# Stores, low parts, norms and reloads moved within the attention and gate stages of a hybrid encoder block

## The chip, the cores and the metric

The kernel runs on one core of a Trainium2 chip. The metric is the device time of one execution in microseconds (us). The engines of the core run side by side, each working through its own queue in order: TensorE (PE in the profile; its weight loads are PEld), VectorE (DVE), ScalarE (ACT), GpSimd (POOL), and SyncE (SP), which here issues nearly all DMAs. An instruction that waits holds up everything behind it on its own queue and nothing else, except through the data and the buffers that others wait for.

## What is computed

One layer of a bidirectional hybrid encoder over 1024 tokens of width 1024, in float32:

```python
h = rmsnorm(x, norm_mix)
q, k, v, r, lr_f, lr_b, u, g_a, g_b = split(h @ w_in)
# branch A: gated linear attention, 4 heads, forward and backward scan, summed
log_a = log_sigmoid(lr @ w_decay_up + b_decay) / 16           # one for each direction
o = gla(q, k, v, log_a_f) + flip(gla(flip(q), flip(k), flip(v), flip(log_a_b)))
o = o * rsqrt(mean(o * o) + eps) * gla_norm                   # for each head
y_a = (o * silu(r)) @ w_branch_gla
# branch B: window means of u minus the token, a small product per group
merged = sigmoid(g_a) * y_a + sigmoid(g_b) * y_b
x = x + merged @ w_out
x = x + (silu(gate) * up) @ w_ffn_out                         # gate, up = rmsnorm(x) @ w_ffn_in
out = rmsnorm(x, norm_final)
```

## The kernel before

**Products.** Every float32 matrix product is made of three matmuls on operands that are split into a high part (`hi`, a cast on ACT) and a low part (`lo`, source minus `hi`, on DVE or POOL): `hi*hi`, `lo*hi`, `hi*lo` (`split_to`, L200 to L202; `products`, L270 to L273). A group of three is called a unit here. After each group `mm3` calls `pump` (L162), which issues whatever side work has come due: steps put off by `soon(delay, step)` (a first-in first-out list, counted in units), weight splits in `pending`, a list `aside` of jobs that run beside the products, and `side`, generators that issue the attention. So the order of each queue is fixed when the program is written, and a unit on PE is the clock by which the other engines' work is dealt out.

**Larger products** such as the projections of r, of the gates and of the feed-forward part run in a form with seven block products instead of eight (`p` = 1 to 7). It needs sums of blocks of the weights and of the activations beforehand. `branch_jobs` and `r_jobs` make such sums of weights on POOL (the tiles `wsum` and `rraw`, recorded at L755), store them to DRAM (L736) and are dealt out by `prepare_beside(jobs, every, ...)` (L767): one step for each `every` units, only while no weight split is pending, and with `floor` as the limit for how far a late job list may catch up. A job's store is issued three steps after the job.

**Heads.** For head 0 to 3 the loop at L1186 makes q and k (`project_qk`, L882) while the attention of the head before runs in `side`. After head 0 come three value products and `store_block`, which writes one block of the features to DRAM so that its buffers can be used for other things; then the two job lists are started (L1198, L1199). After head 2 come the value products of heads 2 and 3.

**Attention of a head** (`attention`, L913). First the decays: four products `z`, for each a DVE step (`la`, L925) and an ACT step (absolute value, L926), then four exponentials (L931), then four logarithms (L940). Between these, the previous head's second half is finished (`unscaled`, L932 to L936): `norm` (L1092, two DVE instructions for each part) and `turn` (L1099, a DVE transpose), which lays out the head's output in a tile `ot` and puts four stores for each half on the list `deferred`. `flush` (L938) issues what is on that list on the SP queue: eight stores, four of the half that was turned in the loop and four of the half that was turned just before. Then come scans and exponentials (`decay`, `exponentials`, `apply_decay` with two POOL products, L985 and L986), the backward states, and the loop over eight chunks (L1118), which has on PE the output products and the next state, on DVE the state update (L1016) and the copy of the output (L1132), on ACT the scaled states (`sf`, L1023) and the sum of squares (L1133). At chunks 5, 6 and 7 of that loop the first half of the head's own output is normed and turned (L1145 to L1151). The last head isn't turned (L1100); its second half is normed after the loop by `soon` (L1156). That output is read much later, by `gated` in the first gate run.

**The r products** (L1399): 21 block products of 12 matmuls, n = 0 to 20, three units `u` for each of `p` = 2, 5, 3, 1, 6, 7, 4, beside the attention of the last head. Before each, `r_step` splits the weights that are needed four products later and loads those of seven later, and `r_event(n)` issues what is listed at L1380 to L1397. Each product's result is read out of its PSUM bank (`r_evict`, L1360) by ACT (L1369) or added by DVE (L1367); p = 5 needs the right-hand operand `right[5]`, a sum of features whose high part is cast by `cast_sum` (L699, ACT) and whose low part is made by `low_sum` (L704) as `trl`. That of p = 5 is put off from inside the k projection of the last head (L907). Three PSUM banks go round among the projections and the r products, so product n waits until the bank of three before has been read. Products 18 to 20 have p = 4 and add into the banks that p = 7 used, so each waits for the DVE addition of the product three before.

At events 14 to 23 the stored outputs of heads 0 to 2 are loaded again (`load_ol`), r rows go through a silu (`gate_row`) and are multiplied on DVE (L1313). At events 20 and 21 `load_block_again` fetches the block that `store_block` had put away, as high and low part (`hh`, `hl`), four loads of 512 KB. The first gate run follows the r products (its p order is 1, 5, 6, 3, 2, 7) and uses the reloaded block for p = 2.

**Buffers.** Most tiles of 4 KB for each partition share a pool of 39 slots; a DMA or a cast into a new tile waits until an earlier tile's last reader is done. Weight parts share pools of 4 raw and 6 split buffers.

Of the kernel before, what the change touches and what calls it, by code (L numbers as in the profile page):

```python
# [23 lines left out]
HEADS = 4  # L24
# [30 lines left out]
def kernel(  # L55
# [20 lines left out]
    nc = tc.nc  # L76
# [21 lines left out]
    def slot(dtype=F32, shape=(2, HALF), s="slot"):  # L98
        return slots.tile([P, *shape], dtype, tag="slot", name=name(s))
# [55 lines left out]
    def soon(delay, *steps):  # L155
        put_off.extend([delay, step] for step in steps)
# [101 lines left out]
    def take(ahead=True):  # L258

        if not ready:  # L260
            prepare()
        w = ready.pop(0)
        w.finish()
        if ahead:
            prepare()
        return w
# [291 lines left out]
    def later(dst, src):  # L558
        deferred.append((dst, src))

    def flush(eng=nc.sync):
        while deferred:
            eng.dma_start(*deferred.pop(0))
# [78 lines left out]
    def r_jobs():  # L642
        raws = {}
        todo = [(u, c) for u in range(TRIO + 1) for c in range(2)]

        def load_rows_of(u, c):
            raws[u, c] = slot(s="rraw")
            for j in range(2):
                k0, c0 = (4 * j + 2 * c) * P, R0 + 2 * u * P
                nc.sync.dma_start(  # L650
                    raws[u, c][:, j, :].rearrange("p (k x) -> p k x", k=2),
                    w_in[k0 : k0 + 2 * P, c0 : c0 + 2 * P].rearrange("(k p) x -> p k x", p=P),
                )

        yield partial(load_rows_of, *todo[0]), None, None
        for n, (u, c) in enumerate(todo):
            if n + 1 < len(todo):
                yield partial(load_rows_of, *todo[n + 1]), None, None
            halves = [raws[u, c][:, j, :].rearrange("p (k x) -> p k x", k=2) for j in range(2)]
            a11, a12, a21, a22 = (halves[j][:, :, i * P : (i + 1) * P] for i in range(2) for j in range(2))  # L660
            for op, dst, a, b, p in (
                (padd, a22, a21, a22, 5), (psub, a21, a11, a21, 7), (psub, a11, a22, a11, 6), (psub, a12, a12, a11, 3)
            ):
                yield partial(op, dst, a, b), None, r_out[u][p][:, 2 * c : 2 * c + 2, :]
# [29 lines left out]
    def load_sums(p):  # L694
        sums_in[p] = [slot(F32R, s="trl")[:, :, :] for _ in range(2)]
        for c, t in enumerate(sums_in[p]):
            nc.sync.dma_start(as_f32(t), f_out[p][:, c])
# [69 lines left out]
    def prepare_beside(jobs, every, put=PUT, lag=1, quick=0, floor=-1e9):  # L767
        aside.append([beside(chain(*jobs), every, put, lag, quick), 1 if quick else every, floor])
# [97 lines left out]
    def r_step():  # L866
        n = next(r_steps, None)
        if n is not None:
            r_split(n)
            r_load(n + 3)  # L870
        return n is not None
# [10 lines left out]
    def project_qk(h, last=False):  # L882
        q = slot(s="q")
        k = slot(s="k")
        for dst, scale in ((q, DK**-0.5), (k, 1.0)):
            final = last and dst is k
            w = take(not final)
            if final:
                value_weights[0].splits(2)
            elif last:  # L890
                value_weights.append(ValueWeights())
            begun = h == HEADS - 1 and dst is k
            if begun:
                load_sums(5)
                for _ in range(2):
                    r_step()
            for half in range(2):
                ps = feature_major(w, hT, half)
                nc.scalar.activation(dst[:, half, :], ps[:, :], AF.Copy, scale=scale)
                if begun:  # L900
                    r_step()
                    if half == 0:
                        load_sums(6)
                        for c in range(2):
                            cast_sum(5, c)
                        for c in range(2):
                            soon(4 + 2 * c, partial(low_sum, 5, c))  # L907
                elif h == HEADS - 1 and half == 0:
                    for n in range(3):
                        r_load(n)  # L910
        qk_heads[h] = q, k

    def attention(h):  # L913
# [21 lines left out]
        if unscaled:  # L935
            unscaled.pop(0)()  # L936
        yield 1.5
        flush()  # L938
        for run in runs:
            nc.scalar.activation(zs[run][:, :], zs[run][:, :], AF.Ln, bias=1.0)  # L940
        yield 6.5

        totals = {}

# [147 lines left out]
        def norm(half, part):  # L1092
            for i in range(2 * part, 2 * part + 2):
                t = o[half][:, i, :]
                nc.vector.scalar_tensor_tensor(
                    t, t, scales[half][:, i : i + 1], gain_row[:, :], op0=ALU.mult, op1=ALU.mult
                )

        def turn(half, part):  # L1099
            if h == HEADS - 1:  # L1100
                return
            if part == 0:
                turned[half] = slot(shape=(DV // SQ, 4 * SQ), s="ot")
            two = slice(2 * part, 2 * part + 2)
            nc.vector.transpose(
                turned[half][:, :, :].rearrange("p k (n b) -> p n k b", b=SQ)[:, two],
                o[half][:, two, :].rearrange("p n (k a) -> p n k a", a=SQ),
            )
            if part:
                to = o_out[h][half].rearrange("(k a) (i m) -> i a k m", a=SQ, i=4)  # L1110
                for i in range(4):
                    later(to[i], turned[half][i * SQ : (i + 1) * SQ, :, :])
# [5 lines left out]
        for n in range(NT):  # L1118
            half, i = n // 4, n % 4
            op = bank(ps_g, "op")  # L1120
            products(op[:, :DV], tokens(p, n), value(n), last=False)
            terms = []
            if n < NT - 1:
                terms.append((chunk_of(qe, n, 1), sb[half][:, i, :]))
            if n > 0:
                terms.append((chunk_of(qe, n, 0), sf[:, :]))
            for j, (a, b) in enumerate(terms):
                if j == len(terms) - 1 and n < NT - 1:
                    sf = s1((DV,), "sf")
                    old = advance(old, n, 0, kts[half, 0], sf[:, :], n == NT - 2)  # L1130
                nc.tensor.matmul(op[:, :DV], a, b, start=False, stop=j == len(terms) - 1)
            nc.vector.tensor_copy(o[half][:, i, :], op[:, :DV])  # L1132
            nc.scalar.activation(  # L1133
                op[:, DV:], op[:, :DV], AF.Square, scale=1.0 / 16.0, accum_out=ms[:, n : n + 1]
            )
            if n == 0:
                yield 0.38
                kts[1, 0] = transposed_keys(1, 0)
            if n == 1:
                yield 0.75  # L1140
                q_next = scores(1)
            if n == 3:
                p = q_next
                scales[0] = rms_scale(ms[:, :4], 4, "ors")
            if n == 5:  # L1145
                norm(0, 0)
            elif n == 6:
                turn(0, 0)
            elif n == 7:
                norm(0, 1)  # L1150
                turn(0, 1)  # L1151
            yield 1.02
        scales[1] = rms_scale(ms[:, 4:], 4, "ors")
        if h == HEADS - 1:
            o_heads[h] = o
            for part in range(2):  # L1156
                soon(3 + part, partial(norm_and_turn, part))
            return
        unscaled.extend(partial(norm_and_turn, part) for part in range(2))

# [25 lines left out]
    for h in range(HEADS):  # L1186
        if h:
            project_qk(h, h == 2)
        else:
            first_qk()  # L1190
            begin(attention(0))
        if h < HEADS - 1:
            begin(attention(h + 1))
        if h == 0:
            for ts in ((7,), (6,), (5, 4)):
                pair_products(ts)
            store_block()
            prepare_beside(map(branch_jobs, range(4)), 2.7)  # L1198
            prepare_beside([r_jobs()], 1.5, floor=-0.5)  # L1199
        if h == 2:  # L1200
            value_weights.pop().products()

# [170 lines left out]
    def event(n, *steps):  # L1373
        r_events.setdefault(n, []).extend(steps)
# [16 lines left out]
    for u in range(TRIO):  # L1391
        event(14 + u, partial(load_ol, u, 0))
        event(16 + u, partial(gate_row, u, 0))
        event(18 + u, partial(load_ol, u, 1))
        event(21 + u, partial(gate_row, u, 1))
    event(20, partial(load_block_again, 0))
    event(21, partial(load_block_again, 1))  # L1397

    for n, (u, p) in enumerate(r_products):  # L1399
        if n:  # L1400
# [826 lines left out]
    for at, p in enumerate(OUT_ORDER):  # L2227
# [9 lines left out]
        for i in range(CLOSE if closing else n_of):  # L2237
            n = at * n_of + i
# [57 lines left out]
```

## Time and profile before

| | |
|---|---|
| time, median of 3 runs | 1369.36 us (1368.5 to 1370.36) |
| profiled execution, its own time | 1369.4 us |
| its span, first to last instruction | 1367.7 us |
| DVE, ACT, POOL busy | 854.2, 652.0, 801.8 us |
| DMA | 268.24 MB, mean 196 GB/s |
| mean granted clock of TensorE | 0.997 |

The profile is one execution. A row of a timeline gives the start, the busy time, the engine, the line, the operation with its output and inputs, the count of merged instructions, and in brackets how long the engine had been idle before it and which instruction ended that wait. A row of a table of stretches gives for each engine the busy time and the number of instructions, then the granted clock, the share of the DMA engines' time and GB/s. A row of waits gives the total, the number and the longest in us. Start times of matmuls that follow each other without a gap lie some 0.23 us apart, though each is shown with 0.39 us, since they are pipelined.

### The profile page before, as it was taken

Reading aid. Unit: us, or ns where it says so; the run is one execution under the profiler, and the core shown is the slowest. Engines: PE = TensorE matmul, PEld = TensorE weight load, DVE = VectorE, ACT = ScalarE, POOL = GpSimd, SP = SyncE. Lnnn points to the kernel's source line nnn. Section 1 sums busy time; section 2 is a strip of 40 time slices with the busy share of each in tenths; the row PEclk is TensorE's granted clock in tenths of the full one; section 3 lists DMA queues with packets and bytes.
Section 4 is the critical chain, followed back from the end, with each engine's and each line's share of the span. In section 5 each row is a group of like instructions: output and inputs, shape, how many; then the busy total and the mean of one; then the engine's idle time right before and its main releaser. Section 6 shows DMA issues by size and latency. Waiting matters only on the chain. (4 is left out here: it accounts for less than half of the span.)

```text
span 1367.7 us, 17976 instructions
## 1 busy us (share of the span) xinstructions
PE 1350.2 (99%) x6226; PEld 1123.2 (82%) x6226; DVE 854.2 (62%) x1051; ACT 652.0 (48%) x1184; POOL 801.8 (59%) x608
## 2 busy tenths in 40 slices
PE   9999999999999999999999999999999999999998
PEld 7888887878788888888888888888888888888886
DVE  6975566567435767769874955565565556343375
ACT  7365665676434445554356533333333334444253
POOL 3332846385496547658764386666666667555454
PEclk9999999999999999999999999999999999999999
DMA  7343638454987669996426354555544447975561
GB/s 228 111 162 101 192 105 228 123 157 134 306 278 253 202 186 335 373 372 220 135 77 233 126 172 154 178 177 177 176 157 137 140 142 272 391 286 185 170 215 77
DMA packets 190139, 268.24 MB, mean 196 GB/s; under 512 B 12728, under 2 KB 112608, under 8 KB 190048
## 3 DMA queue, kind: packets, MB, share of 16 engines
q1 hardware_dynamic: 189904, 266.83, 58.3%
q8 instruction: 49, 0.80, 0.2%
q14 instruction: 42, 0.34, 0.1%
q10 hardware_dynamic: 144, 0.26, 0.1%
HBM read 178.70 MB, written 88.34 MB: 195 GB/s over the span
## 5 line engine op out<-in xcount | busy, mean ns | idle before, releaser
L202 POOL TENSOR_TENSOR wl<-fs,wh 128x512 fp32r<-128x512 f32 x120 | 166.2, 1388 | 155.2 <-ACT wh L201 97.9
L273 PE MATMUL ps<-gh,wh 128*128 128x512 f32 x616 | 240.8, 391 | 0.0
L273 PE MATMUL ps<-gl,wh 128*128 128x512 f32 x616 | 240.1, 390 | 0.3 <-DVE gl L1854 0.3
L273 PE MATMUL ps<-gh,wl 128*128 128x512 f32 x616 | 240.0, 390 | 0.0
L202 POOL TENSOR_TENSOR wl<-fraw,wh 128x512 fp32r<-128x512 f32 x90 | 129.6, 1440 | 62.1 <-ACT wh L201 59.7
L202 POOL TENSOR_TENSOR ol<-gor,oh 128x1024 fp32r<-128x1024 f32 (+1 forms) x42 | 101.8, 2428 | 85.5 <-ACT oh L201 70.3
L273 PEld LDWEIGHTS ps<-gl,wh 128*128 128x128 f32 x616 | 115.7, 188 | 24.3 <-DVE gl L1854 0.7
L273 PEld LDWEIGHTS ps<-gh,wl 128*128 128x128 f32 x616 | 115.7, 188 | 24.1
L273 PEld LDWEIGHTS ps<-gh,wh 128*128 128x128 f32 x616 | 115.8, 188 | 23.9 <-ACT hb L1873 0.2
L273 PE MATMUL ps<-hh,wh 128*128 128x512 f32 x296 | 120.3, 407 | 0.1
L273 PE MATMUL ps<-oh,ol 128*128 128x512 f32 x308 | 120.0, 389 | 0.0
L273 PE MATMUL ps<-ol,oh 128*128 128x512 f32 x308 | 119.9, 389 | 0.0
L273 PE MATMUL ps<-oh,oh 128*128 128x512 f32 x308 | 119.9, 389 | 0.0
L202 POOL TENSOR_TENSOR wl<-wraw,wh 128x512 fp32r<-128x512 f32 x56 | 93.3, 1696 | 44.2 <-ACT wh L201 39.3
L273 PE MATMUL ps<-hh,wl 128*128 128x512 f32 x296 | 116.0, 392 | 2.9 <-POOL wl L202 2.9
L273 PE MATMUL ps<-hl,wh 128*128 128x512 f32 x296 | 116.1, 392 | 0.8 <-DMA hl<-h_out 0.8
L202 DVE TENSOR_TENSOR ol<-wor,oh 128x1024 fp32r<-128x1024 f32 (+1 forms) x42 | 62.4, 1496 | 66.9 <-ACT oh L201 53.9
L273 PE MATMUL ps<-trh,wh 128*128 128x512 f32 x224 | 89.1, 398 | 1.9 <-ACT r L1369 1.9
L273 PE MATMUL ps<-trl,wh 128*128 128x512 f32 x224 | 87.3, 390 | 0.0
L273 PE MATMUL ps<-trh,wl 128*128 128x512 f32 x224 | 87.3, 390 | 0.0
L201 ACT CAST wh<-fs 128x512 fp32r<-128x512 f32 x120 | 73.7, 614 | 26.2 <-DVE fs L1223 25.1
L201 ACT CAST oh<-wor 128x1024 fp32r<-128x1024 f32 (+1 forms) x42 | 41.1, 978 | 63.9 <-PE ps L273 26.5
(286 smaller groups left out, 3148.2 us busy)
## 6 DMA issues: line engine op xcount, KB each, us to landing
fraw<-in_w_ffn_in_dram SPq DMA_DIRECT2D x44, 512.0 KB, 7.2
gor<-g_out SPq DMA_DIRECT2D x35, 512.0 KB, 4.9
g_out<-s SPq DMA_DIRECT2D x44, 256.0 KB, 2.4
fraw<-in_w_in_dram SPq DMA_DIRECT2D x20, 512.0 KB, 6.7
wor<-t_out SPq DMA_DIRECT2D x20, 512.0 KB, 4.8
g_out<-g SPq DMA_DIRECT2D x33, 256.0 KB, 2.5
x<-in_x_dram SPq DMA_DIRECT2D x16, 512.0 KB, 4.5
wor<-in_w_ffn_out_dram SPq DMA_DIRECT2D x15, 512.0 KB, 7.8
```

The source lines that it names most:

```text
L201: nc.scalar.copy(hi, src)
L202: eng.tensor_tensor(lo, src, as_f32(hi), op=ALU.subtract)
L273: nc.tensor.matmul(ps, a[i], b[j], start=first and n == 0, stop=last and n == 2, skip_group_check=onto)
```

## The change

Five edits, all in the order in which work is issued; no operation is added or taken out.

1. `flush` of the finished head's stores moves from before the logarithms to behind them and behind 6.5 more units.
2. The two low parts of `right[5]` go from DVE to GpSimd, put off by 3 and 6 units where it was 4 and 6.
3. In the last head the two norms of the first half leave the loop. All four parts are normed after it, at 4, 6, 8 and 10 units; the two of the second half were at 3 and 4.
4. The job lists are dealt out at another pace: `branch_jobs` every 1.6 units with a limit on catching up, where it was 2.7 without one; `r_jobs` every 1.2 where it was 1.5.
5. The block is loaded again at events 18 and 19 instead of 20 and 21; the second loads of `ol` and their rows move one event later.

```diff
@@ project_qk
                         for c in range(2):
-                            soon(4 + 2 * c, partial(low_sum, 5, c))
+                            soon(3 + 3 * c, partial(low_sum, 5, c, nc.gpsimd))
@@ attention
         yield 1.5
-        flush()
         for run in runs:
             nc.scalar.activation(zs[run][:, :], zs[run][:, :], AF.Ln, bias=1.0)
         yield 6.5
+        flush()
...
         def turn(half, part):
-            if h == HEADS - 1:
-                return
             if part == 0:
...
-            if n == 5:
-                norm(0, 0)
-            elif n == 6:
-                turn(0, 0)
-            elif n == 7:
-                norm(0, 1)
-                turn(0, 1)
+            if h < HEADS - 1:
+                if n == 5:
+                    norm(0, 0)
+                elif n == 6:
+                    turn(0, 0)
+                elif n == 7:
+                    norm(0, 1)
+                    turn(0, 1)
             yield 1.02
         scales[1] = rms_scale(ms[:, 4:], 4, "ors")
         if h == HEADS - 1:
             o_heads[h] = o
-            for part in range(2):
-                soon(3 + part, partial(norm_and_turn, part))
+            for part in range(4):
+                soon(4 + 2 * part, partial(norm, part // 2, part % 2))
             return
@@ the loop over heads
             store_block()
-            prepare_beside(map(branch_jobs, range(4)), 2.7)
-            prepare_beside([r_jobs()], 1.5, floor=-0.5)
+            prepare_beside(map(branch_jobs, range(4)), 1.6, floor=-0.5)
+            prepare_beside([r_jobs()], 1.2, floor=-0.5)
@@ the events of the r products
     for u in range(TRIO):
         event(14 + u, partial(load_ol, u, 0))
         event(16 + u, partial(gate_row, u, 0))
-        event(18 + u, partial(load_ol, u, 1))
-        event(21 + u, partial(gate_row, u, 1))
-    event(20, partial(load_block_again, 0))
-    event(21, partial(load_block_again, 1))
+        event(19 + u, partial(load_ol, u, 1))
+        event(22 + u, partial(gate_row, u, 1))
+    event(18, partial(load_block_again, 0))
+    event(19, partial(load_block_again, 1))
```

## The prediction

> **What bounds the kernel.** I read the page's busy times, then PE's waits between 150 and 365 us, where all five edits lie, then the stretches around the longest.
>
> ```profile
> PE 1350.2 (99%) x6226; PEld 1123.2 (82%) x6226; DVE 854.2 (62%) x1051; ACT 652.0 (48%) x1184; POOL 801.8 (59%) x608
> ...
> PE ps L273 <- POOL wl L202: 3.7, 2, 2.9
> PE ps L273 <- ACT r L1369: 1.9, 1, 1.9
> PE op L1131 <- ACT sf L1023: 1.6, 1, 1.6
> PE ps L273 <- DMA hl<-h_out: 0.8, 1, 0.8
> ...
> 220.00:223.00 3.00, 0.27 (x2) 0.00 (x0) 2.38 (x4) 1.11 (x4) 3.00 (x4) 1.00 0.88 275
> 223.00:229.00 6.00, 5.87 (x24) 5.04 (x25) 2.81 (x6) 3.01 (x9) 5.84 (x8) 0.72 0.55 153
> ...
> 800.00:850.00 50.00, 50.00 (x222) 41.42 (x221) 27.61 (x29) 17.53 (x32) 33.02 (x25) 1.00 0.57 179
> ```
>
> PE is the bound, and no edit takes a matmul away. What can be won is PE's waiting: five waits, 8.0 us idle. The true loss is larger in two ways. In the steady part 222 matmuls take 50 us, 0.225 us each, while a row shows 0.39; a wait therefore costs its idle time plus about 0.16 us. And behind the longest wait the granted clock is 0.72 for 6 us, which costs 6 x 0.28 = 1.7 us. Start to start, the losses are, in order of time: 1.0 us (a low part of a value weight, at 166), 3.0 and 1.7 us (a low part for the last head's q, at 220, and the clock behind it), 2.3 us (the bank of the first r product, at 271 to 276), 1.7 us (a scaled state in the last head's loop, at 325) and 1.0 us (the reloaded block, at 360). That is 10.7 us, so nothing much below 1358.7 is to be had. The profiled execution took 1369.4 us, its span 1367.7 and 1.7 around it; that is the median of the runs, so the sum is made against 1369.4.
>
> **The later stores (edit 1) and the q weights at 220.**
>
> ```profile
> 195.93 9.04 POOL L755 TENSOR_TENSOR rraw<-rraw 128x256 f32<-128x256 f32 x11
> ...
> 199.22 7.74 SPq L563 DMA_DIRECT2D o_out<-ot  x8
> ...
> 209.36 0.98 SPq L650 DMA_DIRECT2D rraw<-in_w_in_dram  x2
> ...
> 214.27 0.85 POOL L755 TENSOR_TENSOR rraw<-rraw 128x256 f32<-128x256 f32 x1 [9.30 <-DMA rraw<-in_w_in_dram]
> 215.08 1.29 POOL L985 TENSOR_TENSOR qe<-qe,q 128x512 f32<-128x512 f32 x1
> ...
> 221.81 1.26 POOL L202 TENSOR_TENSOR wl<-raw,wh 128x512 fp32r<-128x512 f32 x1
> ...
> 219.88 0.39 PE L273 MATMUL ps<-hl,wh 128*128 128x512 f32 x1
> 223.13 0.50 PE L273 MATMUL ps<-hh,wl 128*128 128x512 f32 x1 [2.86 <-POOL wl L202]
> ...
> L563 SPq DMA_DIRECT2D o_out<-ot x24: 303/467/1053, 131.1 to 277.7; - x24
> ```
>
> PE wants the low part at 219.88 + 0.23 = 220.1 and gets it at 223.1. POOL is late because it stood 9.3 us waiting for weights, and these were loaded late because SP held the eight stores for 7.7 us, waiting for the last `turn`. Moved back by 6.5 units, the stores no longer stand before that load: it can go once POOL has read what is stored ahead of it, at about 200.5, and lands 4.9 us later (209.36 to 214.27), at 205.4. POOL then does its four sums of that load by 208.7 (9.04 / 11 = 0.82 each). The stores are now ahead of the next load instead: with 0.47 us each they take SP until about 208, that load lands near 213.5.
>
> The faster pace (edit 4) counts against this. Going through the units, before the split for q comes due the old pace has dealt five r sums, the new one eight, while the branch steps go from one in 2.7 with catching up to one in two: 21 instead of 23 before the value products. So POOL does four sums (213.5 to 216.8), a `qe` product with its factor (1.29 + 0.2, to 218.3) and the low part (1.26): 219.6 against 220.1. It just fits. I take a remaining wait of 0.4 us (bounds: 0, and the full 3.0 if the load lands 3.5 us later) and no clock loss, since the waits of 1.87 and 1.60 us left the clock at 1.00 (row of 274 below, for the first). Gain 3.0 + 1.7 - 0.4 = **4.3 us**, from 0 to 4.7. The Trainium skill ("TensorE: Matmul & The Clock Gate", section "Why this matters for your kernels") lets the clock fall only behind idle gaps of more than about 3 us. The 2.86 us here lie just under that; by the rule the 1.7 us need not belong to this wait, and the edit would bring 2.6 us.
>
> For head 0's stores at 131 the same holds, but nothing on PE waits there. For the last head the stores are also issued by the loop of r products at its second product, behind the same loads as now, so the move changes nothing.
>
> **The wait at 166 (edit 4).**
>
> ```profile
> 140.00:166.00 26.00, 26.00 (x131) 21.73 (x130) 17.16 (x29) 18.88 (x40) 23.68 (x20) 1.00 0.73 212
> ...
> 161.66 1.29 POOL L755 TENSOR_TENSOR wsum<-wsum 128x512 f32<-128x512 f32 x1
> ...
> 165.71 2.50 POOL L202 TENSOR_TENSOR wl<-raw,wh 128x512 fp32r<-128x512 f32 x2
> ...
> 167.03 0.50 PE L273 MATMUL ps<-wl,hh 128*128 128x512 f32 x1 [0.85 <-POOL wl L202]
> ```
>
> POOL had been busy for 23.7 of the 26 us up to here, so what counts is what is queued ahead of this split. By the new pace twelve branch steps instead of eleven come before the second head's q and 21 instead of 23 before the value products, so six sums instead of seven lie in that queue: 1.29 us less against 1.0 lost. Gain **0.9 us** (0 to 1.0).
>
> **The low parts on GpSimd (edit 2).**
>
> ```profile
> 263.72 1.22 DVE L706 TENSOR_TENSOR trl<-trl,trh 128x1024 fp32r<-128x1024 f32 x1
> ...
> 266.17 1.22 DVE L706 TENSOR_TENSOR trl<-trl,trh 128x1024 fp32r<-128x1024 f32 x1
> ...
> 268.14 0.66 ACT L926 ACTIVATE z<-z,cols 128x512 f32<-128x512 f32 x1 [1.19 <-DVE la L925]
> 268.73 2.04 ACT L931 ACTIVATE z<-z 128x512 f32<-128x512 f32 x4
> ...
> 275.52 0.63 ACT L1369 COPY r<-ps 128x512 f32<-128x512 f32 x1
> ...
> 276.21 0.50 PE L273 MATMUL ps<-trh,wh 128*128 128x512 f32 x1 [1.87 <-ACT r L1369]
> ...
> 274.00:276.30 2.30, 0.43 (x3) 0.09 (x1) 1.97 (x3) 2.30 (x6) 0.40 (x1) 1.00 0.90 224
> ...
> 300.72 2.39 POOL L706 TENSOR_TENSOR trl<-trl,trh 128x1024 fp32r<-128x1024 f32 x1
> ```
>
> The fourth r product waits for ACT to empty the first one's bank. ACT is late because its absolute values wait for DVE's `la`, between which the two low parts stand. Without these 2.44 us the `la` and the absolute values end about 2.2 us earlier (the last `z` product allows no more), ACT starts its exponentials near 266.5 instead of 268.73, and the bank is free at 273.9 instead of 276.15. PE, itself 0.27 us earlier, would start at 273.9. Gain **2.0 us** of 2.3 (bounds 0.3, if only the small wait at 271 goes, and 2.3). On POOL each part takes 2.39 us: from about 264 to 269, before the split of the fourth product's weights and well before the product reads them. Late next is the DVE norm of head 2, which has all its inputs in SBUF and may have to go between POOL's instructions; its result is only stored, and the scans behind it wait for the logarithms.
>
> **The norms behind the loop (edit 3).**
>
> ```profile
> 321.93 3.51 DVE L1095 SCALAR_TENSOR_TENSOR o<-o,ors,gain_row 128x256 f32<-128x256 f32 x2
> ...
> 326.43 0.70 PE L1131 MATMUL op<-sf,qe 128*128 128x256 f32 x2 [1.60 <-ACT sf L1023]
> ...
> 327.51 0.87 DVE L1095 SCALAR_TENSOR_TENSOR o<-o,ors,gain_row 128x256 f32<-128x256 f32 x2
> ...
> 329.58 4.78 DVE L1095 SCALAR_TENSOR_TENSOR o<-o,ors,gain_row 128x256 f32<-128x256 f32 x4 [0.53 <-POOL ors L305]
> ...
> 335.48 4.07 DVE L706 TENSOR_TENSOR trl<-trl,trh 128x1024 fp32r<-128x1024 f32 x2
> 339.48 1.28 DVE L1313 TENSOR_TENSOR r<-ol,r 128x512 f32<-128x512 f32 x2
> 340.68 0.68 DVE L1367 TENSOR_TENSOR r<-ps,r 128x512 f32<-128x512 f32 x1
> ```
>
> Two norms that take 0.87 us alone took 3.51 beside POOL, and the state update stood behind them: this 1.7 us of PE goes. But behind the loop DVE is full until 341, and the addition at 340.68 is the one that product 19 waits for already: product 18 has just ended. Four norms come into that stretch. I follow the queue in times relative to PE: the first half's four, partly beside POOL's splits, fill the pauses up to 334.0, two more come before the second addition, and the low parts start at 335.5, as now. The last two norms then stand ahead of the products of L1313 and the addition, which ends 0.9 us later. Gain 1.7 - 0.9 = **0.8 us**; with every norm at the 4.78 / 4 = 1.2 us of the row it is a loss (below), with none of it late 1.7.
>
> **The earlier reload (edit 5).**
>
> ```profile
> 348.53 0.33 SPq L718 DMA_DIRECT2D hh<-h_out  x1
> ...
> DMA to landing us min/median/max: 8.8/8.8/8.9
> ...
> 360.48 0.50 PE L273 MATMUL ps<-hl,wh 128*128 128x512 f32 x1 [0.81 <-DMA hl<-h_out]
> 362.99 1.29 POOL L202 TENSOR_TENSOR wl<-fraw,wh 128x512 fp32r<-128x512 f32 x1 [6.90 <-ACT wh L201]
> ```
>
> Two products earlier are about 5 us: landing near 355 instead of 360.4. Four of the 39 slots are taken sooner; counting tiles, 35 are in use there. The `ol` loads that give way go to rows which DVE multiplies with 6 us to spare. Late next is the first gate unit's split at 363.0; PE doesn't wait for it now, and its load will share the DMA with less. Gain **0.9 us** (0.5 to 1.0).
>
> **The sum.** 0.9 + 4.3 + 2.0 + 0.8 + 0.9 = 8.9 us; 1369.4 - 8.9 = **1360.5 us**.
>
> **Rivals.** (a) The q weights stay late: the load behind the stores lands 3.5 us later, as the eight loads and stores around it share a DMA busy to 0.88, and the eight sums stand ahead. 1360.5 + 4.3 = 1364.8; chance 0.17. (b) DVE doesn't keep up behind the loop: each norm takes 1.2 us, the low parts of p = 4 end 2 us later, the addition for product 19 at 345.9 instead of 341.4. PE then loses 4.5 us where I put 0.9: 1364.1, or 1365.8 with a fall of the clock. For it: the rows of 3.51 and 4.78. Against: the first half's norms find DVE idle. Chance 0.15. The Trainium skill ("GPSIMD Engine Reference", section 8, "Key points") has GpSimd contend with every DVE instruction that has two SBUF inputs, which is this rival; its section 4.1 would leave the low parts on DVE too, at half the time (rows: 1.22 against 2.39). (c) The clock falls at 223 without the wait: 1360.5 + 1.7 = 1362.2; chance 0.05. The clock gate page's 3 us give this case. (d) The edits do what they say but POOL is the bound: its longer queue keeps the waits of 166 and 220 and holds the low parts: only 0.9 us remain, 1368.5; chance 0.09. (e) Slower: the stores, now between the r loads, hold the second one. Each us that it lands later than 214 is one more on PE. Break-even is a landing near 222, and at 225, with 1.05 us for each store and a slow landing, the low part comes 11 us late: 11.0 + 1.7 - 4.7 - 4.6 = 3.4 us more, 1372.8. Against: a store's median is 0.47 us, and 4.9 us the landing seen here. Chance 0.06.
>
> **How the numbers follow.** My forecast has 0.48, with its own range from 1358.6 to 1362. Faster by over 0.2% (2.7 us, about what a measurement of this kernel tells from no change) are the forecast, (a), (b) and (c): 0.85. Within 0.2% is (d): 0.09. Slower is (e): 0.06. The range takes in (a), (b) and (c): 1358.4 to 1366.4.
>
> **What would show it.** Right: no PE wait on `wl` at 166 and 220 and a clock of 1.00 behind it; POOL's wait for `rraw` gone; the L1369 copy some 2 us earlier against PE; no wait on `sf`, but one of about 1 us for L1367 at product 19; none on `hl`. Wrong: `wl` still ends PE's wait at the last head's q, or a wait of over 3 us in the r products.

## The result and the profile after

The changed kernel takes 1367.47 us (median of 20 runs, 1366.24 to 1368.5) against 1369.9 us before (20 runs on the same chip, 1368.11 to 1371.58): a ratio of 0.9981, 95% interval 0.9974 to 0.9988. It is faster, by 2.4 us and not by 8.9, and the time lies above the range that was given. The span of the profiled execution fell from 1367.7 to 1365.8 us.

First the page's busy times and PE's waits of the changed kernel (engine, line waited for, then total, number and longest in us):

```profile
PE 1350.0 (99%) x6226; PEld 1122.7 (82%) x6226; DVE 851.9 (62%) x1049; ACT 651.2 (48%) x1184; POOL 809.9 (59%) x610
...
PE ps L273 <- POOL wl L202: 4.5, 3, 4.2
...
PE ps L273 <- DVE r L1366: 0.8, 1, 0.8
PE ps L273 <- DVE ga L1642: 0.4, 1, 0.4
```

The waits on ACT's bank copy, on `sf` and on the reloaded `hl` have left the list, as was forecast. The wait on `wl` has stayed and its longest piece has grown from 2.9 to 4.2 us. Where it lies, and what follows it, show PE's timeline and the table of stretches (busy time of PE, PEld, DVE, ACT, POOL, then granted clock, DMA share, GB/s):

```profile
170.36 0.80 PE L273 MATMUL ps<-wl,hh 128*128 128x512 f32 x1 [4.15 <-POOL wl L202]
...
225.41 0.39 PE L273 MATMUL ps<-hl,wh 128*128 128x512 f32 x1
226.02 0.50 PE L273 MATMUL ps<-hh,wl 128*128 128x512 f32 x1 [0.22 <-POOL wl L202]
...
339.48 0.50 PE L273 MATMUL ps<-trh,wh 128*128 128x512 f32 x1 [0.76 <-DVE r L1366]
```

```profile
166.00:170.20 4.20, 0.21 (x1) 0.00 (x0) 0.11 (x1) 1.31 (x3) 4.20 (x5) 0.77 0.86 229
170.20:176.00 5.80, 5.64 (x23) 5.29 (x24) 1.94 (x4) 1.84 (x4) 5.64 (x7) 0.58 0.52 196
...
225.00:231.00 6.00, 5.78 (x31) 4.67 (x30) 4.71 (x8) 2.29 (x7) 5.92 (x6) 1.00 0.54 154
274.00:276.30 2.30, 2.29 (x10) 1.60 (x9) 2.19 (x4) 2.30 (x6) 0.47 (x1) 1.00 0.97 279
```

The long wait is no longer at 220 but at 166, at the low part of the value weight, where it was 0.85 us; behind it the clock is 0.58 for 5.8 us. At 220 (here 226, since PE comes later) 0.22 us are left and the clock is 1.00.

Both kernels issue the same 6226 matmuls in the same order, so the start of each one can be set against its own start before. The matmul at 219.88 in the kernel before (shown in the prediction) starts at 225.41 in the changed one, for example: PE is 5.5 us behind there. From 20 us on this lag changes at the following places, and nowhere else by more than 0.1 us (times of the kernel before; us gained, a loss with a minus):

| place | measured | as predicted |
|---|---|---|
| 166 to 172: value weight's low part, and the clock behind it | -5.5 | 0.9 |
| 220 to 229: last head's q, and the clock behind it | 4.2 | 4.3 |
| 271 to 276: bank of the first r product | 2.2 | 2.0 |
| 325 to 342: `sf` (1.9), then product 19 (-0.8) | 1.1 | 0.8 |
| 355 to 374: reload, first gate units | -0.1 | 0.9 |
| sum | 1.9 | 8.9 |

Three places (220, 271, 325) came out within 0.3 us of their terms. The first ate nearly three quarters of what these brought. Its cause can be read off two queues. First SP's timeline around head 0's stores, before:

```profile
131.09 9.05 SPq L563 DMA_DIRECT2D o_out<-ot  x8
140.24 6.75 SPq L795 DMA_DIRECT2D raw<-in_w_in_dram  x5
...
149.54 1.02 SPq L597 DMA_DIRECT2D wsum<-in_w_branch_gla_dram  x2
```

and SP's, then GpSimd's, after:

```profile
136.91 10.12 SPq L795 DMA_DIRECT2D raw<-in_w_in_dram  x5
147.09 4.69 SPq L563 DMA_DIRECT2D o_out<-ot  x8
...
152.39 0.38 SPq L795 DMA_DIRECT2D raw<-in_w_in_dram  x1
...
153.55 1.06 SPq L597 DMA_DIRECT2D wsum<-in_w_branch_gla_dram  x2
```

```profile
161.17 1.29 POOL L755 TENSOR_TENSOR wsum<-wsum 128x512 f32<-128x512 f32 x1 [5.82 <-DMA wsum<-in_w_branch_gla_dram]
...
169.04 2.50 POOL L202 TENSOR_TENSOR wl<-raw,wh 128x512 fp32r<-128x512 f32 x2
```

The eight stores used to be followed by the value-weight loads, which wait for buffers until 147 in any case. Now those loads come first and the stores stand behind them, ahead of the branch-sum load, with only one more weight load and two stores of sums between: it goes 4.0 us later (149.54 to 153.55). GpSimd, which had no pause there, stands for 5.82 us, and the split of the value weight, queued behind those sums, starts at 169.04 instead of 165.71.

### The profile page after: what moved, and what is told of

It reads as the page before. It is cut to its first block, busy times and chain, and to the rows that moved or that the text cites. A ratio compares the mean times of both kernels' runs of the same rounds, so it can differ in the third digit from the quotient of the medians.

```text
span 1365.8 us, 17979 instructions
## 1 busy us (share of the span) xinstructions
PE 1350.0 (99%) x6226; PEld 1122.7 (82%) x6226; DVE 851.9 (62%) x1049; ACT 651.2 (48%) x1184; POOL 809.9 (59%) x610
```

## Experiments

Theory 1: the place of head 0's stores, in front of the branch-sum load, made the value weight late. Theory 2: the new pace of the job lists did. A third, that late stores hurt by themselves, was added later. All medians are in us; each ratio is to the kernel before, run beside it.

### 1. Head 0's stores back in their place, all else as changed

```diff
+        if h == 1:
+            flush()
         for run in runs:
             nc.scalar.activation(zs[run][:, :], zs[run][:, :], AF.Ln, bias=1.0)
         yield 6.5
-        flush()
+        if h > 1:
+            flush()
```

> All five edits, but the stores of head 0 are issued where they were, ahead of the logarithms; those of heads 1 and 2 stay late. Theory 1 (the eight stores moved in front of the branch-sum load at 150 made the value weight late): the wsum load goes at about 149.5 instead of 153.55, GpSimd's pause of 5.8 us goes, the wait of PE at 166 falls from 4.2 us to under 1, the clock behind it stays at 1.00: 5.5 us less than the changed kernel, 1362.0. Theory 2 (the new pace of the branch sums made it late): the wait stays at 3 us or more, 1367.

Measured: 1362.7, ratio 0.9940 (0.9925 to 0.9955). SP, GpSimd, PE and the stretch behind the wait:

```profile
149.03 0.94 SPq L597 DMA_DIRECT2D wsum<-in_w_branch_gla_dram  x2
```

```profile
157.37 1.29 POOL L755 TENSOR_TENSOR wsum<-wsum 128x512 f32<-128x512 f32 x1 [1.82 <-DMA wsum<-in_w_branch_gla_dram]
```

```profile
167.55 0.50 PE L273 MATMUL ps<-wl,hh 128*128 128x512 f32 x1 [0.69 <-POOL wl L202]
...
170.20:176.00 5.80, 5.58 (x28) 4.33 (x27) 4.10 (x9) 3.49 (x9) 5.03 (x4) 1.00 0.38 142
```

The load goes at 149.03, GpSimd's pause shrinks from 5.82 to 1.82 us, PE's from 4.15 to 0.69, and the clock stays at 1.00. As theory 1 has it.

### 2. The old pace of both job lists, all else as changed

```diff
-            prepare_beside(map(branch_jobs, range(4)), 1.6, floor=-0.5)
-            prepare_beside([r_jobs()], 1.2, floor=-0.5)
+            prepare_beside(map(branch_jobs, range(4)), 2.7)
+            prepare_beside([r_jobs()], 1.5, floor=-0.5)
```

> The changed kernel with the old pace of both job lists. Theory 1: the wsum load is still at about 153.5 and the wait at 166 is still 3 to 4.5 us with a lower clock behind it; 1367 to 1368. Theory 2: the wait at 166 is 1 us again, 1362.

Measured: 1367.9, ratio 0.9979 (0.9970 to 0.9989). SP's load and PE's wait:

```profile
153.51 1.07 SPq L597 DMA_DIRECT2D wsum<-in_w_branch_gla_dram  x2
```

```profile
170.46 0.80 PE L273 MATMUL ps<-wl,hh 128*128 128x512 f32 x1 [4.30 <-POOL wl L202]
```

Nothing changes at 166: theory 2 falls. At the last head's q the old pace leaves PE no wait at all, so the edit isn't needed there either.

### 3. The later stores alone

The kernel before with `flush()` behind `yield 6.5`.

> The kernel before with the later stores alone (edit 1). Theory 1: 166 loses 5 us more, as in the changed kernel, and 220 wins about 4.3: 1369 to 1371. Theory 2: 166 stays at 1.0 and 220 wins 4.3: 1365.6.

Measured: 1372.76, ratio 1.0016 (1.0006 to 1.0025): slower, and above the 1371 of theory 1. PE at 166, and the stretches around 220:

```profile
170.67 0.80 PE L273 MATMUL ps<-wl,hh 128*128 128x512 f32 x1 [4.28 <-POOL wl L202]
...
218.00:224.00 6.00, 6.00 (x30) 4.97 (x29) 5.40 (x11) 4.68 (x11) 5.84 (x8) 1.00 0.98 282
224.00:230.00 6.00, 6.00 (x34) 5.14 (x33) 4.68 (x9) 2.32 (x6) 5.92 (x7) 1.00 0.48 134
```

The edit brings what was forecast for the last head (PE is busy throughout, 4.7 us won between 220 and 229) and loses 6.0 us at 166 to 172. Of the rest, 1.6 us in this profile are a fall of the clock near 280, which is taken up under the hardware.

### 4. The new pace alone

The kernel before with the two lines of pace of the change.

> The kernel before with the new pace alone (edit 4). Theory 1: 166 within 1 us of before, and 220 as before or, with eight r sums instead of five ahead of its split, up to 2.5 us later: 1369 to 1372. Theory 2: 166 loses 5 us: 1374 or more.

Measured: 1372.49, ratio 1.0014 (1.0005 to 1.0024): slower. At 166 PE loses 0.85 us where it lost 1.01, but two new losses of 0.45 and 0.48 us stand beside it, at 161 and 175, where PE waits for low parts that DVE makes (`kt` and `p`). At the last head's q:

```profile
225.05 0.79 PE L273 MATMUL ps<-hh,wl 128*128 128x512 f32 x1 [3.52 <-POOL wl L202]
...
225.00:231.00 6.00, 5.95 (x18) 4.98 (x19) 1.68 (x4) 1.61 (x4) 5.84 (x7) 0.52 0.55 146
```

The pace doesn't make the wait at 166, and with the stores in their old place it makes the one at 220 longer (2.86 to 3.52 us of idle time), by the eight r sums instead of five that come ahead of the split.

### 5. The low parts on GpSimd alone

```diff
-                            soon(4 + 2 * c, partial(low_sum, 5, c))
+                            soon(3 + 3 * c, partial(low_sum, 5, c, nc.gpsimd))
```

> The kernel before with the low parts on GpSimd alone (edit 2). If the chain la, absolute values, exponentials, bank is what the fourth r product waits for, the 2.3 us lost between 270 and 276 go down to 0 to 0.3 without any help of the other edits: 1369.9 - 2.0 to 2.3 = 1367.6 to 1367.9. If the wait in the changed kernel went only because the stages ahead of it had moved against each other, 1 us or more of it stays: 1368.7 or above.

Measured: 1367.96, ratio 0.9980 (0.9970 to 0.9989). The stretch in which PE was busy for 4.22 of 6 us before has no wait left:

```profile
270.00:276.00 6.00, 5.99 (x27) 4.66 (x26) 5.82 (x8) 5.97 (x12) 3.42 (x3) 1.00 0.41 110
```

The 2.3 us go without any other edit: the chain from `la` to the bank was the cause.

### 6. The norms behind the loop alone

The kernel before with edit 3.

> The kernel before with the norms behind the loop alone (edit 3). As priced: the 1.7 us at 325 (PE on sf) go, 0.9 us on the addition L1367 before product 19 come: 0.8 less, 1369.1. The rival, every norm at 1.2 us: 1372.

Measured: 1368.99, ratio 0.9991 (0.9982 to 1.0000). The wait on `sf` is gone, and this one has come:

```profile
341.98 0.50 PE L273 MATMUL ps<-trh,wh 128*128 128x512 f32 x1 [0.76 <-DVE r L1366]
```

Start to start that is 0.92 us, as priced, and the rival with norms of 1.2 us each has fallen. The timing agrees but can't tell 0.8 us from nothing by itself.

### 7. The earlier reload alone

The kernel before with edit 5.

> The kernel before with the earlier reload and the later ol loads alone (edit 5). As priced: the 1.0 us at 360 (PE on hl) go: 1369.0. The rival, seen in the changed kernel as waits of 0.4 us at the first gate unit's low part and split: 0.3 to 0.7 of it come back there, 1369.3 to 1369.6, within what the timing can tell.

Measured: 1370.26, ratio 0.9998 (0.9989 to 1.0007). PE has no wait on `hl`, but two small gaps where the first gate units begin, at the second of each of these pairs of rows:

```profile
356.66 0.39 PE L273 MATMUL ps<-trh,wl 128*128 128x512 f32 x1
357.14 0.50 PE L273 MATMUL ps<-hh,wh 128*128 128x512 f32 x1
...
372.10 0.39 PE L273 MATMUL ps<-trh,wl 128*128 128x512 f32 x1
372.61 0.50 PE L273 MATMUL ps<-trh,wh 128*128 128x512 f32 x1
```

Over the usual 0.23 us they lose 0.25 and 0.28 us. With the smaller gaps just behind them, matmul for matmul, 0.8 us come back of the 1.1 that the wait on `hl` cost, and 0.3 remain, which the timing can't show.

### 8. Stores of head 0 back, and the old pace

Experiment 1 with the pace of experiment 2, so edits 2, 3, 5 and the later stores of heads 1 and 2.

> The first experiment (stores of head 0 back in their place) with the old pace of both job lists too, so edits 2, 3, 5 and the late stores of heads 1 and 2. If the pace is worth nothing once the stores stand right: 1362.7 within 0.7, a wait of about 1 us at 166 and none over 0.4 at 220. If it is needed for the low part at 220: a wait of 2 us or more there, 1364 or above. If it brings the 0.9 us at 166 that was predicted: 1363.6.

Measured: 1361.52, ratio 0.9936 (0.9920 to 0.9953). PE at 166:

```profile
167.31 0.50 PE L273 MATMUL ps<-wl,hh 128*128 128x512 f32 x1 [0.91 <-POOL wl L202]
```

With no wait at 220 either, the pace is worth nothing that can be measured: without it the kernel is no slower than in experiment 1. Experiment 1 has the same two small losses near 161 and 175 as experiment 4 (0.5 us each); here, with the old pace, they are gone.

### 9. Head 0's stores later still, behind the load

All five edits, and:

```diff
         yield 6.5
-        flush()
+        if h == 1:
+            soon(8, flush)
+        else:
+            flush()
```

> All five edits, and head 0's stores put off by 8 units more, so that the branch-sum load stands just ahead of them instead of just behind. Theory 1 (what hurts is the place in front of that load): the wsum load goes at about 149 to 150, the wait at 166 is 1 us or less and the clock stays at 1.00, though the stores are later than in any other kernel: 1362.7 within 0.7, as with the stores put back. Rival (what hurts is that the stores move beside the value products at all, by the traffic or by SP): the load still lands near 161 and the wait stays at 2 us or more, 1365 or above.

Measured: 1362.01, ratio 0.9940 (0.9927 to 0.9954). SP, GpSimd and PE:

```profile
148.94 0.94 SPq L597 DMA_DIRECT2D wsum<-in_w_branch_gla_dram  x2
149.98 6.55 SPq L563 DMA_DIRECT2D o_out<-ot  x8
```

```profile
156.28 1.30 POOL L755 TENSOR_TENSOR wsum<-wsum 128x512 f32<-128x512 f32 x1 [0.81 <-DMA wsum<-in_w_branch_gla_dram]
```

```profile
166.49 0.50 PE L273 MATMUL ps<-wl,hh 128*128 128x512 f32 x1 [0.19 <-POOL wl L202]
...
177.34 0.70 PE L1132 MATMUL op<-sf,qe 128*128 128x256 f32 x2 [0.82 <-ACT sf L1026]
```

This is the sharpest of the tests: the stores are later than in the changed kernel, and the loss at 166 is gone, because two positions in SP's queue are exchanged. Being late does no harm here; standing in front of that load does. The wait on `sf` at 177 is new and wasn't followed further.

### 10. The last two norms behind the additions

Experiment 8, and the second half's norms leave the list of put-off steps for event 20:

```diff
-            for part in range(4):
-                soon(4 + 2 * part, partial(norm, part // 2, part % 2))
+            for part in range(2):
+                soon(4 + 2 * part, partial(norm, 0, part))
+            last_norms.extend(partial(norm, 1, part) for part in range(2))
...
+    event(20, lambda: [step() for step in last_norms])
```

> The best kernel so far (stores of head 0 in their old place, old pace) with the last two norms issued at event 20 of the r products, behind the addition that product 19 waits for. If these norms are what makes that addition late: the 0.93 us at product 19 go, 1360.6. If the low parts ahead of it do: it stays, 1361.5.

Measured: 1360.29, ratio 0.9927 (0.9913 to 0.9940), the fastest of all. The wait on the addition at product 19 isn't on PE's list any more: these two norms made it, not the low parts ahead of them. (The wait at 166 is 1.6 us in this profile, where experiments 8 and 11, the same up to there, have 0.9 and 0.8: a difference of that size at this place says nothing.) Against the changed kernel's ratio of 0.9981 the intervals lie far apart.

### 11. The reload one event later

Experiment 10 with the reload at events 19 and 20, and the `ol` loads and rows where they were before the change.

> The kernel with the last two norms at event 20, and the block reloaded one event earlier than in the kernel before (19 and 20) with the ol loads and their rows where they were there. If the 0.7 us lost at the first gate copy come from the ol loads moved back (the copy waits for a buffer that the product of ol and r gives free): they go, and the reload still lands in time or up to 0.3 us late: 1359.9 to 1360.3. If they come from the reload itself: they stay, 1360.6.

Measured: 1361.46, ratio 0.9936 (0.9923 to 0.9948), not to be told from experiment 10. The gap at the first gate copy did not go, it grew from 0.4 to 1.2 us; a second one some 16 us behind it (0.6 us in experiment 10) went, so that the two changes about cancel. ACT's timeline:

```profile
346.80 0.59 ACT L1642 COPY ga<-ps 128x512 f32<-128x512 f32 x1 [3.78 <-DMA ob_out<-r]
```

The copy waits for the store of a finished r row. That store frees a buffer, and in experiments 1, 8 and 10 the same copy is released by the last product that reads an `ol` tile; so it reads as a shortage of the shared buffers rather than of anything in the `ol` loads. This was read from the releasers and not tested with another number of buffers.

### 12. Experiment 10 with head 0's stores behind the load

Here the old pace deals the steps, so the stores come one position later than in experiment 9, behind another store.

> The kernel with the last two norms at event 20 and the old pace, and head 0's stores not in their old place but put off until they stand behind the branch-sum load. If that place is better for the value weight, as with the new pace (0.3 us lost at 166 instead of 0.8): 1359.5 to 1360. If GpSimd's queue alone sets the low part under the old pace: 1 to 1.8 us lost at 166 as before, 1360.3.

Measured: 1364.56, ratio 0.9961 (0.9947 to 0.9974), worse than either answer. SP, ACT and PE:

```profile
151.46 7.74 SPq L563 DMA_DIRECT2D o_out<-ot  x8
```

```profile
160.50 0.59 ACT L201 CAST kt<-kp 128x512 fp32r<-128x512 f32 x1 [6.79 <-DMA o_out<-ot]
```

```profile
161.14 0.39 PE L273 MATMUL kv<-vh,kt 128*128 128x256 f32 x1 [3.46 <-ACT kt L201]
```

Issued 1.5 us later than in experiment 9, the stores end after the cast of `kt` needs a buffer that an `ot` tile still holds; ACT stands for 6.79 us and PE for 3.46. So of the places tried for head 0's stores two are good, ahead of the value-weight loads and just behind the branch-sum load; 1.5 us later is too late already.

## Why the prediction was wrong, step by step

**Edit 1 at head 0: the step that failed.** The prediction says "For head 0's stores at 131 the same holds, but nothing on PE waits there." The first half of that sentence is what happened: as at the next head, the stores moved from ahead of one load to ahead of another. The second half was read from the profile before, in which that other load (the branch sum's) was in time and so was nobody's wait. But the prediction itself quotes GpSimd as busy for 23.7 of 26 us ahead of the value weight, with the low part already 0.85 us late: a queue without slack, fed by just that load. Of the load's delay of 4.0 us, 3.3 reached the split and PE, and the clock of 0.58 behind the longer wait took 2.2 more: 5.5 us lost where a gain of 0.9 was forecast. Experiments 1, 3 and 9 show it from three sides. The rival (e) had the mechanism, stores that hold up a load, but put it at the r loads alone and its chance at 0.06.

**Edit 1 at 220.** Forecast 4.3 us, 4.2 came. The load landed at 219.28 and GpSimd reached the low part at 224.68, with PE some 5.5 us later than before; on the clock of before that is 213.8 and 219.2, where 213.5 and 218.3 were worked out:

```profile
219.28 3.34 POOL L755 TENSOR_TENSOR rraw<-rraw 128x256 f32<-128x256 f32 x3 [0.69 <-DMA rraw<-in_w_in_dram]
...
224.68 1.29 POOL L202 TENSOR_TENSOR wl<-raw,wh 128x512 fp32r<-128x512 f32 x1
```

Rival (a) did not occur, and without the wait the clock stayed up, so (c) did not either: the 1.7 us behind the 2.86 us did belong to that wait. In all the profiles without it the clock is 1.00 there, in all with it 0.50 to 0.72 over the six microseconds from 223.

**Edit 4.** Forecast 0.9 us; it is worth nothing (experiments 2 and 8) and costs by itself (experiment 4), in part by the two small losses beside the value weight. One sum fewer does stand ahead of the value weight's split, but in experiment 1 GpSimd then waits 1.82 us for the next weights, more than the 1.29 us of a sum: with a shorter queue the landing of the load became the bound. Only with the stores behind the load (experiment 9) does the wait shrink, to 0.19 us.

**Edits 2 and 3.** Forecast 2.0 and 0.8; 2.2 and 1.1 came, and experiments 5 and 6 show them apart. The follow-on loss at product 19 was forecast at 0.9 us and is 0.8; experiment 10 shows that it comes from the last two norms. Rival (b) fell.

**Edit 5.** The wait on `hl` went as forecast, but the term of 0.9 us was wrong: nothing is left of it in the changed kernel, and 0.3 us alone. What the wait had cost came back at the first gate units. The prediction counted 35 of 39 buffers in use and looked for trouble at the split; the copies of `ga` were late instead, and experiment 11 points to the buffers.

**The sum.** 1367.5 lies close to rival (d)'s 1368.5, but by another way: GpSimd was not the bound, it stood idle for 5.8 us, and the wait at 220 went. Of the 7.0 us between forecast and result, 6.4 are at the value weight (5.5 lost and 0.9 not won), 1.0 at the reload and 0.1 at 220; the bank and the norms brought 0.5 more than forecast.

## What to carry to other kernels

When a block of DMAs is moved in an in-order queue, write down for every place where it occurs which load stands behind it before and which after, and follow that load to the engine that reads it; that nobody waited for it in the old profile says only that it was in time there. A queue that is 90% busy and ends in a wait of PE has no slack for a late input, so price any delay of its inputs in full, the clock behind the wait included. And a store that is put off has a far end as well: the buffer that it reads is wanted by somebody.

## What the runs showed of the hardware

The granted clock fell behind some short pauses of PE and not behind others of the same length. The wait for the bank of the first r product stands in the kernel before (1.87 us, shown in the prediction) and in experiments 3, 4, 6 and 7. Here are, of experiment 3, its row and the stretch behind it:

```profile
277.71 0.50 PE L273 MATMUL ps<-trh,wh 128*128 128x512 f32 x1 [1.83 <-ACT r L1369]
...
279.00:283.00 4.00, 4.00 (x13) 3.22 (x12) 2.51 (x6) 3.97 (x8) 4.00 (x4) 0.65 0.92 247
```

and the same stretch in the kernel before:

```profile
279.00:283.00 4.00, 4.00 (x19) 3.30 (x19) 2.58 (x6) 3.99 (x8) 4.00 (x4) 1.00 0.78 200
```

With 1.83 us of idle time the clock was 0.65 over these four microseconds, with 1.87 us it was 1.00. Of the other three profiles experiment 6 has 0.75 there, experiments 4 and 7 have 1.00, all after 1.8 to 1.9 us. The prediction had taken the one case that it saw as a sign that waits below 2 us leave the clock alone, and the row that it named for this (274.00 to 276.30) ends 0.1 us after the wait and says nothing of the time behind it. Behind the waits of 2.86, 3.52 and 4.15 us shown in the rows above and in the prediction it was 0.72, 0.52 and 0.58, over some 6 us. The Trainium skill ("TensorE: Matmul & The Clock Gate", section "What's actually happening") has the gate judge activity in a window of about 3.4 us that runs freely, so that the same work can meet it differently. That equal pauses fared differently agrees with this; that one of 1.83 us, far shorter than such a window, lowered the clock at all does not agree with its table, which asks for a whole idle window, and here the measurement decides.
